# Decoder trunk on one core: every fourth weight chunk's low part comes from an accumulating GpSimd DMA

## The chip, the core and the metric

The kernel runs on one core of one Trainium2 chip. The metric is the device time of one execution in microseconds (us). The engines are TensorE (PE in the profile, its weight loads PEld), VectorE (DVE), ScalarE (ACT), GpSimd (POOL) and SyncE (SP). Each works through a queue of its own in order, and they wait for each other with semaphores. DMAs are issued from the queues of SyncE, ScalarE and GpSimd.

## What is computed

A decoder trunk of two layers over 256 tokens of width 2048, all in float32. A layer is a mixer (one input projection of 5632 columns; sliding-window attention with sinks beside a gated linear recurrence; one output projection), a SwiGLU feed forward of width 5632, and a gated per-layer embedding, with RMS norms between:

```python
for i in range(DEPTH):                     # 2
    h = rms_norm(x, pre_mix_gain[i])
    m = hybrid_mixer(h, positions, w_in[i], ..., w_out[i])
    x = x + rms_norm(m, post_mix_gain[i])
    h = rms_norm(x, pre_ffn_gain[i])
    f = (jax.nn.silu(h @ w_ffn_gate[i]) * (h @ w_ffn_up[i])) @ w_ffn_down[i]
    x = x + rms_norm(f, post_ffn_gain[i])
    gate = jax.nn.sigmoid(rms_norm(x, ple_gain[i]) @ w_ple_gate[i])
    x = x + (p[i] @ w_ple_proj[i]) * gate
```

## The kernel before

Every large product has its two operands split into a high and a low part of at most 12 significant bits each (type fp32r), and is made of three products: high by high, low by high, high by low. Lines 206, 207 and 208, in `part` inside `strip`, are these three; their accumulators are the tiles `acc`, two of them per strip, one for each token tile of 128 tokens. A strip is 512 output columns for both token tiles. It walks over its weights in chunks of two k-tiles of 512 columns (128 x 1024 elements, 512 KB), eight chunks to a strip of 2048 rows; a chunk feeds 12 matmuls. There are 840 chunks in the program.

`load_w` brings a chunk in. Its DMA on SyncE's queue (L188) writes a tile `wr`, of which there are four buffers. `split` then lets ScalarE cast it to the high part `wh` (L159), and VectorE subtract that from `wr` to give the low part `wl` (L160). Of `wh` and `wl` there are eight buffers each. So a load waits until a `wr` buffer has been read by VectorE, and a cast waits until TensorE has done with the `wh` buffer of eight chunks earlier. The inputs of the products, tiles `ck`, are made by `split_T`: TensorE transposes (L167, `ms`), ScalarE writes the high part (L175, with a gain, or L159), VectorE the low one (L176 or L160).

A scheduler that works before the launch sets the order on each engine and the buffer that each tile gets; it takes the instructions in the order of the program text, and moves one ahead when it estimates that it will be ready sooner. The text itself delays work by chunks: `later(n, fn)` writes a piece n chunks on.

Around the strips stand the pieces that take the accumulators away: rotary halves (VectorE L395, GpSimd L402), attention and recurrence, the activations of the feed forward (L697, L703), the running sum of the down projection (L721, L723), and `post_norm`, which at the end of the two output projections of a layer adds the normed result to the residual `x` (L232) and makes the next inputs. Sums of squares are ScalarE's (L155, tile `junk`), and the few steps from them to a reciprocal root are GpSimd's (L140 to L150). In the strips that follow a norm, `skew` makes the second token tile run four or five chunks behind the first.

Of the kernel before, what the change touches and what calls it, by code (L numbers as in the profile page):

```python
# [8 lines left out]
F32 = mybir.dt.float32  # L9
# [27 lines left out]
    0.0003162277571391314, 0.00023713737027719617, 0.00017782794020604342, 0.0001333521504420787,  # L37
]
PI = 3.141592653589793
BIG = (25600.0, 134.0, 1.921875, 0.005126953125, 1.6254460206255317e-05)  # 4096 * 2 pi  # L40
TWO = (6.28125, 0.0019350051879882812, 3.0199157663446385e-07)  # 2 pi
ROUND = 12582912.0  # 1.5 * 2^23


@with_exitstack
def decoder(ctx: ExitStack, tc: tile.TileContext, x, p, positions, w_in, attn_sinks,
# [19 lines left out]

    queue = []
    clock = [0]

    def later(n, fn):  # L70
        """trace fn n weight chunks from now"""
        queue.append((clock[0] + n, fn))

    running = []

    def start(gen):
        """trace gen up to its first yield, and from one yield to the next every chunk"""
        running.append(gen)
        if next(gen, True):
            running.remove(gen)  # L80
# [13 lines left out]
    def bank(shape=(P, W)):  # L94
        return pms.tile(list(shape), F32, tag="ms", name="ms")

# [1 line left out]
    xr = [[xp.tile([P, W], F32, tag=f"x{t}{s}", name=f"x{t}{s}") for s in range(4)]  # L98
          for t in range(NT)]
# [1 line left out]
    ident = cp.tile([P, P], F32, name="ident")  # L101
    make_identity(nc, ident)
    mhalf = cp.tile([P, 8], F32, name="mhalf")
    G.memset(mhalf, -0.5)

    # per-feature vectors, one feature per partition
    g0rows = cp.tile([32, P], F32, name="g0rows")
    S.dma_start(g0rows, pre_mix_gain.rearrange("l (c p) -> (l c) p", p=P))
    gT = cp.tile([P, P], F32, name="gT")
# [21 lines left out]
    def gain_cols(base, l, n):  # L131
        return gT[:, base + l * n: base + (l + 1) * n]

# [1 line left out]
    def rstd(ss, n, count=1, name="rs"):  # L135
        """(ss / n + eps) ^ -0.5, ss [P, count]"""
        v = tiny(count)
        V.tensor_scalar(v, ss, 1.0 / n, EPS, op0=ALU.mult, op1=ALU.add)
        r = sm.tile([P, count], F32, name=name)
        G.tensor_tensor(r, v, mhalf[:, 0:count], op=ALU.pow)  # L140
        return r
# [13 lines left out]
        S.activation(j[:, 0:shape[1]], src, AF.Square, accum_out=acc)  # L155

    def split(src, hi, lo):
        """src = hi + lo, each of at most 12 significant bits"""
        S.copy(hi, src)  # L159
        V.tensor_tensor(lo, src, hi.bitcast(F32), op=ALU.subtract)  # L160

    def split_T(src_blocks, gcols, hl, t, kt0=0):
        """transpose 128-wide blocks [tok, feat] and split, per-feature gain if given"""
        n = len(src_blocks)
        ps = bank((P, n, P))
        for b, blk in enumerate(src_blocks):
            T.transpose(ps[:, b], blk, ident)  # L167
        h = hl[0][:, kt0:kt0 + n, t * P:(t + 1) * P]
        lo = hl[1][:, kt0:kt0 + n, t * P:(t + 1) * P]
        if gcols is None:  # L170
            split(ps, h, lo)
            return
        for b in range(n):
            g = gcols[:, b:b + 1]
            S.activation(h[:, b], ps[:, b], AF.Copy, scale=g)  # L175
            V.scalar_tensor_tensor(lo[:, b], ps[:, b], g, h[:, b].bitcast(F32),  # L176
                                   op0=ALU.mult, op1=ALU.subtract)
# [5 lines left out]
        return [a[:, b * P:(b + 1) * P] for b in range(4)]  # L183

    def load_w(w, c, col):
        """two k-tiles of 512 columns, split"""
        raw = wpr.tile([P, 2, W], F32, tag="wr", name="wr")
        nc.sync.dma_start(raw, w[c * 2 * P:(c + 1) * 2 * P, col:col + W].rearrange(  # L188
            "(k p) n -> p k n", p=P))
        hi = wps.tile([P, 2, W], F32R, tag="wh", name="wh")  # L190
        lo = wps.tile([P, 2, W], F32R, tag="wl", name="wl")
        split(raw, hi, lo)
        return hi, lo

    def strip(lhs, w, col, done, nch=8, row0=0, skew=0, psum=None, pre=None):
        """512 output columns for both token tiles; lhs[c] = (hi, lo) of 4 k-tiles"""
        ps = psum or [pacc.tile([P, W], F32, tag="acc", name=f"acc{t}") for t in range(NT)]
        ws = {}

        def part(t, c):  # L200
            hi, lo = ws[c]
            for k in range(2):
                kt = 2 * c + k
                xh, xl = (a[:, kt % 4, t * P:(t + 1) * P] for a in lhs[kt // 4])
                first, last = kt == 0, kt == 2 * nch - 1
                T.matmul(ps[t], xh, hi[:, k], start=first, stop=False)  # L206
                T.matmul(ps[t], xl, hi[:, k], start=False, stop=False)  # L207
                T.matmul(ps[t], xh, lo[:, k], start=False, stop=last)  # L208

        for i in range(nch + skew):  # L210
            if pre:
                pre(i)
            if i < nch:
                ws[i] = load_w(w, row0 // (2 * P) + i, col)
                part(0, i)
                if i == nch - 1:
                    done(0, ps[0])
            if i >= skew:
                part(1, i - skew)
            tick()  # L220
        done(1, ps[1])
# [4 lines left out]
        return b  # L226

    def post_norm(mg, ss, t, nss, xT, gcols):
        """after the last strip of a token tile: x += mg * rstd, and the next input"""
        r = sum_rstd(ss[t], D, f"po{t}")  # L230
        for c in range(4):
            V.scalar_tensor_tensor(xr[t][c], mg[c][:, t], r[:, 0:1], xr[t][c],  # L232
                                   op0=ALU.mult, op1=ALU.add)
            next_in(t, c, xT, gcols)
        for c in range(4):
            square_sum(xr[t][c], nss[t][:, c:c + 1])
# [13 lines left out]
            return got[t]  # L250
        return get

    # ---- masks, sinks and rotary tables
    ones = cp.tile([P, P], F32, name="ones")
    m_low = cp.tile([P, P], F32, name="m_low")      # [j, i]: i >= j
    m_up = cp.tile([P, P], F32, name="m_up")        # [j, i]: i < j
    m_prev = cp.tile([P, P], F32, name="m_prev")    # [i, j]: j > i
    m_neg = cp.tile([P, P], F32, name="m_neg")      # [i, j]: j > i gives the mask value
    LEV = (1, 2, 4, 8, 16, 32, 64)  # block lengths; the last two take no mask
    m_lev = cp.tile([P, 5, 64], F32, name="m_lev")  # L260
    lb = cp.tile([P, DEPTH, 8], F32, name="lb")
    omlb = cp.tile([P, DEPTH, 8], F32, name="omlb")
# [8 lines left out]
    def constants():  # L271
# [12 lines left out]
        for li, k in enumerate(LEV[:5]):  # L284
            select(m_lev[:, li], ones[:, :64], [[-2 * k, 64 // k], [0, k]], 0, 1)
            select(m_lev[:, li], m_lev[:, li], [[2 * k, 64 // k], [0, k]], k - 1, -1)
        # lower bounds: softmax over the layers, cumulative sum minus the first
        lmax = tiny(8)
        V.tensor_copy(lmax, lbl[:, 0])
        for l in range(1, DEPTH):  # L290
# [16 lines left out]
            V.tensor_tensor(lb[:, l], lcum, lbl[:, 0], op=ALU.subtract)  # L307
            V.tensor_scalar(omlb[:, l], lb[:, l], -1.0, 1.0, op0=ALU.mult, op1=ALU.add)

        # attention sinks, on every partition  # L310
        G.dma_start(sink.rearrange("p l h -> p (l h)"),
                    attn_sinks.rearrange("l h -> (l h)").partition_broadcast(P))
        V.tensor_scalar(nsink, sink, -1.0, None, op0=ALU.mult)

        # rotary angles: token per partition
        G.dma_start(posi, positions.rearrange("o (t p) -> p (o t)", p=P))
        posf = tiny(NT)
        V.tensor_copy(posf, posi)
# [31 lines left out]
        V.tensor_scalar(ra, ra, -1.0, PI / 2, op0=ALU.mult, op1=ALU.add)  # L350
        S.activation(cos, ra, AF.Sin)

# [1 line left out]
    ss = new_ss("ssx")  # L354
    xT = [new_ck() for c in range(4)]

# [9 lines left out]
            later(4, constants)  # L366

    for l in range(DEPTH):
        # ================= mixer =======================================================
        rx = lazy_rstd(ss, "rx")  # L370
        wi = w_in[l]
        attn = [new_ck(), new_ck()]
# [15 lines left out]
            return rot[t]  # L388

        def rotate(src, tb, i, n, o1, o2):  # L390
            """src [P, n heads, 64] in PSUM; o1, o2: [P, n/4, 4, 32] views in the order (g, j)"""
            a = nat()
            b = nat()
            for d, k in ((a, i), (b, i + 1)):
                V.tensor_tensor(d[:, 0:n * 64].rearrange("p (h d) -> p h d", d=32),  # L395
                                src.rearrange("p (h d) -> p h d", d=32),
                                tb[:, k].unsqueeze(1).to_broadcast([P, 2 * n, 32]), op=ALU.mult)
            av = a[:, 0:n * 64].rearrange("p (g j two d) -> p g j two d", j=4, two=2, d=32)
            bv = b[:, 0:n * 64].rearrange("p (g j two d) -> p g j two d", j=4, two=2, d=32)
            for dst, x1, x2, op in ((o1, av[:, :, :, 0], bv[:, :, :, 1], ALU.subtract),  # L400
                                    (o2, av[:, :, :, 1], bv[:, :, :, 0], ALU.add)):
                G.tensor_tensor(dst, x1, x2, op=op)  # L402
# [51 lines left out]
                    split_T(blocks4(ao[t][:, h]), gain_cols(96, l, 8)[:, 4 * h:4 * h + 4], attn[h], t)  # L454

        def head_group(half, g, t):
            """four query heads on one key head: scores; then the exponentials' transpose; then values"""
            kv = 2 * half + g
            rows = slice(g * 64, (g + 1) * 64)
            q = qT[half]  # L460
# [49 lines left out]
            square_sum(dst, ssa[t][:, kv:kv + 1], (P, 256))  # L510

        class Rec:
            """four heads of the gated recurrence"""

            def __init__(s, grp):
                s.grp = grp
# [145 lines left out]
            strip(xT, wi, 3584 + grp * W, rec.done_i)  # L662
            strip(xT, wi, 4608 + grp * W, rec.done_g)

        # ---- output projection, post norm
        mixT = [mix[c] for c in range(4)]
        ssm = new_ss("ssm")
        ss = new_ss("ssx")
# [11 lines left out]
                    post_norm(mg, ssm, t, ss, xT, gain_cols(32, l, 16))  # L680
            strip(mixT, w_out[l], s * W, done, skew=SKEW if s == 3 else 0)

        # ================= feed forward ================================================
        rx2 = lazy_rstd(ss, "ry")
        ssf = new_ss("ssf")
        nss = new_ss("ssx")
# [44 lines left out]
            ff0 += glen  # L731
        xT, ss = nxT, nss

        # ================= gated per-layer embedding ===================================
        rp = lazy_rstd(ss, "rp")
        pT2 = sp.tile([P, 2, 2, SEQ], F32R, tag="at", name="pT2")
        pT = [pT2[:, 0], pT2[:, 1]]
# [58 lines left out]
```

## Time and profile before

| | |
|---|---|
| time, median of 3 runs | 2515.0 us (2514.89 to 2515.26) |
| span of the profiled execution | 2514.3 us, within 0.7 us of that median; the page gives no other time of this execution |
| granted TensorE clock, mean | 0.999 |
| TensorE / VectorE / ScalarE / GpSimd busy | 99% / 57% / 47% / 4% |
| weight queue of SyncE (q1) | 449.37 MB, 55.9% of the 16 DMA engines' span |

A group line of the profile has the source line, engine, operation and tiles, shapes and count; then busy time and the mean of one in ns; then the idle time of the engine ahead of it and what ended it. A line of waits has who waited for whom, the sum in us, how often, and the longest. A row of windows has its bounds, its length, busy us of each engine with counts, the granted clock, the mean share of the DMA engines and GB/s. A row of the timeline or of the chain has start and duration. The rows themselves stand in the prediction.

### The profile page before, as it was taken

What the parts mean: (1) busy time and instruction counts of PE and PEld (TensorE: products, weight loads), DVE (VectorE), ACT (ScalarE), POOL (GpSimd) and SP (SyncE); (2) the same over time, 40 slices, a digit from 0 to 9 for tenths busy, and PEclk for the clock granted to TensorE, in tenths of its full rate; (3) what the DMA queues carried; (4) which work ended last, traced back from release to release, by engine and by line L of the source; (5) the groups of instructions that cost most, each with busy time, mean ns of one, the idle gap of its engine ahead of it and who ended that gap; (6) DMA issues with size and microseconds to landing.
All of it is one profiled execution on the core that took longest, in us unless ns stands there. A gap on an engine that the chain in (4) does not pass through costs nothing.

```text
span 2514.3 us, 31017 instructions
## 1 busy us (share of the span) xinstructions
PE 2490.2 (99%) x11779; PEld 2063.0 (82%) x11779; DVE 1431.4 (57%) x1777; ACT 1179.4 (47%) x1682; POOL 95.5 (4%) x209
## 2 busy tenths in 40 slices
PE   8999999999999999999999999999999999999999
PEld 6888888888888888887888888888888888888877
DVE  6666655544455455457566766565445544554574
ACT  6554445544444434446555443464444344344463
POOL 2100001000000000001011000010000000000010
PEclk9999999999999999999999999999999999999999
DMA  7344455656556656564563454556666665566653
GB/s 253 126 135 150 152 176 167 212 190 192 191 189 190 192 192 193 185 202 167 179 202 108 151 159 143 191 163 212 189 192 192 190 189 191 193 189 193 200 177 125
DMA packets 234260, 451.43 MB, mean 180 GB/s; under 512 B 14176, under 2 KB 15104, under 8 KB 234112
## 3 DMA queue, kind: packets, MB, share of 16 engines
q1 hardware_dynamic: 233808, 449.37, 55.9%
q8 instruction: 92, 1.51, 0.2%
q14 instruction: 56, 0.46, 0.0%
q10 hardware_dynamic: 240, 0.07, 0.0%
q0 software_dynamic: 64, 0.02, 0.0%
HBM read 447.31 MB, written 2.10 MB: 179 GB/s over the span
## 4 chain that ended last, share of the span: by engine, by line
PE 93%; ACT 2%; DVE 2%; DMA 1%; POOL 1%; issue 1%; SPq 0%; DVEq 0%; ACTq 0%; POOLq 0%
PE acc L206 29%; PE acc L208 29%; PE acc L207 29%; PE ms L579 1%; PE ms L167 1%; ACT junk L155 1%; PE ms L464 1%; ACT ck L175 1%; DVE wl L160 1%; ACT wh L159 1%; DMA wr<-in_w_in_dram 1%; PE ms L505 1%; DMA wr<-in_w_ple_gate_dram 0%; PE ms L594 0%; PE ms L491 0%
## 5 line engine op out<-in xcount | busy, mean ns | idle before, releaser
L160 DVE TENSOR_TENSOR wl<-wr,wh 128x1024 fp32r<-128x1024 f32 x840 | 1029.8, 1227 | 974.8 <-ACT wh L159 954.0
L159 ACT CAST wh<-wr 128x1024 fp32r<-128x1024 f32 x840 | 884.7, 1054 | 1189.2 <-PE acc L207 1127.0
L206 PE MATMUL acc<-wh,ck 128*128 128x512 f32 x3328 | 1309.2, 394 | 5.0 <-ACT ck L175 5.0
L208 PE MATMUL acc<-wl,ck 128*128 128x512 f32 x3328 | 1301.3, 391 | 0.4 <-DVE wl L160 0.4
L207 PE MATMUL acc<-wh,ck 128*128 128x512 f32 x3328 | 1299.9, 391 | 0.0
L206 PEld LDWEIGHTS acc<-wh,ck 128*128 128x128 f32 x3328 | 626.3, 188 | 134.0 <-ACT ck L175 7.6
L208 PEld LDWEIGHTS acc<-wl,ck 128*128 128x128 f32 x3328 | 625.9, 188 | 131.6 <-DVE wl L160 1.6
L207 PEld LDWEIGHTS acc<-wh,ck 128*128 128x128 f32 x3328 | 626.3, 188 | 126.3 <-DVE ck L160 0.5
L175 ACT ACTIVATE ck<-ms,gT 128x128 fp32r<-128x128 f32 x256 | 82.6, 379 | 30.8 <-DVE ck L176 26.1
L176 DVE SCALAR_TENSOR_TENSOR ck<-ms,gT,ck 128x128 fp32r<-128x128 f32 x256 | 79.0, 345 | 17.4 <-ACT ck L175 17.0
L145 POOL TENSOR_TENSOR tiny<-ssf 128x1 f32<-128x1 f32 x4 | 2.1, 534 | 1378.2 <-ACT junk L155 1377.9
L579 PEld LDWEIGHTS ms<-q,k 128*128 128x128 f32 x320 | 38.2, 191 | 2.7 <-PE acc L208 1.7
L579 PE MATMUL ms<-q,k 128*128 128x64 f32 x320 | 38.3, 272 | 0.0
L167 PE MATMUL ms<-ident,x 128*128 128x128 f32 x192 | 31.3, 287 | 5.1 <-DVE x L232 4.1
L697 ACT ACTIVATE nat<-acc,ry 128x512 f32<-128x512 f32 x44 | 30.2, 686 | 10.7 <-PE acc L208 10.6
L155 ACT ACTIVATE junk<-x 128x512 f32<-128x512 f32 x48 | 30.5, 636 | 9.2 <-DVE x L232 3.9
L167 PEld LDWEIGHTS ms<-ident,x 128*128 128x128 f32 x192 | 23.0, 146 | 14.4 <-issue 5.4
L723 DVE TENSOR_TENSOR macc<-acc,macc 128x512 f32<-128x512 f32 x48 | 33.0, 687 | 0.7
L703 DVE SCALAR_TENSOR_TENSOR nat<-acc,ry,nat 128x512 f32<-128x512 f32 x44 | 32.4, 748 | 0.1
L160 DVE TENSOR_TENSOR ck<-ms,ck 128x512 fp32r<-128x512 f32 x44 | 30.1, 684 | 0.0
L481 ACT ACTIVATE nat<-nat,tiny 128x128 f32<-128x128 f32 x64 | 24.9, 390 | 9.0 <-DVE tiny L478 9.0
L402 POOL TENSOR_TENSOR nat<-nat 128x256 f32<-128x256 f32 (+1 forms) x24 | 23.6, 1012 | 140.5 <-PE acc L208 77.9
(184 smaller groups left out, 889.6 us busy)
## 6 DMA issues: line engine op xcount, KB each, us to landing
wr<-in_w_in_dram SPq DMA_DIRECT2D x176, 512.0 KB, 3.5
wr<-in_w_ffn_gate_dram SPq DMA_DIRECT2D x176, 512.0 KB, 3.5
wr<-in_w_ffn_up_dram SPq DMA_DIRECT2D x176, 512.0 KB, 3.5
wr<-in_w_ffn_down_dram SPq DMA_DIRECT2D x176, 512.0 KB, 3.7
wr<-in_w_out_dram SPq DMA_DIRECT2D x64, 512.0 KB, 3.7
wr<-in_w_ple_gate_dram SPq DMA_DIRECT2D x64, 512.0 KB, 4.2
wr<-in_w_ple_proj_dram SPq DMA_DIRECT2D x8, 512.0 KB, 4.6
x<-in_x_dram SPq DMA_DIRECT2D x8, 256.0 KB, 5.3
```

Source lines behind the costliest of these rows:

```text
L155: S.activation(j[:, 0:shape[1]], src, AF.Square, accum_out=acc)
L159: S.copy(hi, src)
L160: V.tensor_tensor(lo, src, hi.bitcast(F32), op=ALU.subtract)
L167: T.transpose(ps[:, b], blk, ident)
L175: S.activation(h[:, b], ps[:, b], AF.Copy, scale=g)
L176: V.scalar_tensor_tensor(lo[:, b], ps[:, b], g, h[:, b].bitcast(F32), op0=ALU.mult, op1=ALU.subtract)
L206: T.matmul(ps[t], xh, hi[:, k], start=first, stop=False)
L207: T.matmul(ps[t], xl, hi[:, k], start=False, stop=False)
L208: T.matmul(ps[t], xh, lo[:, k], start=False, stop=last)
L579: T.matmul(pl[:, t * 4 + h].rearrange("p (b k) -> p b k", k=k), s.k[:, h, t * P:(t + 1) * P], up, start=True, stop=True)
L703: V.scalar_tensor_tensor(gate[t], ps, rx2(t)[:, 0:1], gate[t], op0=ALU.mult, op1=ALU.mult)
L723: V.tensor_tensor(m, ps, m, op=ALU.add)
```

## The change

A counter `nload` numbers the chunks. For three of four nothing changes. For every fourth one (indices 3, 7, 11 and so on) ScalarE makes the high part as before, then ScalarE also writes its negative into `lo`, and a DMA on GpSimd's queue adds the whole `raw` chunk onto it. VectorE has no part in these 210 chunks. Beside that the changed file has its comments removed; line numbers after the counter are one higher, and in `load_w` and after it up to seven higher.

```diff
+    nload = [0]
 ...
         hi = wps.tile([P, 2, W], F32R, tag="wh", name="wh")
         lo = wps.tile([P, 2, W], F32R, tag="wl", name="wl")
-        split(raw, hi, lo)
+        nload[0] += 1
+        if nload[0] % 4:
+            split(raw, hi, lo)
+        else:
+            S.copy(hi, raw)
+            S.mul(lo, hi.bitcast(F32), -1.0)
+            G.dma_start(lo, raw, accum_op=ALU.add)
         return hi, lo
```

Two places of the order, both in the feed forward of the first layer. Numbers at names tell buffers apart, and a bracket has the semaphores that a row waits for: DMAHW of SyncE's and ScalarE's DMAs, DMASW of GpSimd's, the others of engines.

ScalarE, before:

```order
L159 CAST wh_7248<-wr_7246 128x1024 [waits DMAHW7_49,DVE_49,PE_49]
L159 CAST wh_7270<-wr_7268 128x1024 [waits DMAHW0_49,DVE_49,PE_49]
L159 CAST wh_7288<-wr_7286 128x1024 [waits DMAHW1_49,DVE_49,PE_49]
L159 CAST wh_7306<-wr_7304 128x1024 [waits DMAHW2_49,DVE_49,PE_49]
L159 CAST wh_7324<-wr_7322 128x1024 [waits DMAHW3_49,DVE_49,PE_49]
```

ScalarE, after; the chunks of `wr_6854` and `wr_6927` are fourth ones:

```order
L197 CAST wh_6856<-wr_6854 128x1024 [waits DMAHW7_49,PE_49]
L198 ACTIVATE wl_6857<-wh_6856 128x1024 [waits DMASW4_49,PE_49,Activation_49]
L160 CAST wh_6875<-wr_6873 128x1024 [waits DMAHW0_49,DVE_49,PE_49]
L160 CAST wh_6893<-wr_6891 128x1024 [waits DMAHW1_49,DVE_49,PE_49]
L160 CAST wh_6911<-wr_6909 128x1024 [waits DMAHW2_49,DVE_49,PE_49]
L197 CAST wh_6929<-wr_6927 128x1024 [waits DMAHW3_49,PE_49]
```

The multiplication stands right behind its cast and ahead of the next chunk's cast.

SyncE's loads, before:

```order
L188 DMA wr_6804<-in_w_ffn_gate_dram 128x2x512 [waits DMAHW4_49,DVE_49]
L188 DMA wr_6822<-in_w_ffn_gate_dram 128x2x512 [waits DMAHW5_49,DVE_49]
L188 DMA wr_6840<-in_w_ffn_gate_dram 128x2x512 [waits DMAHW6_49,DVE_49]
L188 DMA wr_6858<-in_w_ffn_gate_dram 128x2x512 [waits DMAHW7_49,DVE_49]
L188 DMA wr_6882<-in_w_ffn_up_dram 128x2x512 [waits DMAHW0_49,DVE_49]
```

After, from one fourth chunk to the load that takes its buffer:

```order
L189 DMA wr_6854<-in_w_ffn_gate_dram 128x2x512 [waits DMAHW4_49,DVE_49]
L189 DMA wr_6873<-in_w_ffn_gate_dram 128x2x512 [waits DMAHW3_49,DMASW5_49]
L189 DMA wr_6891<-in_w_ffn_gate_dram 128x2x512 [waits DMAHW5_49,DVE_49]
L189 DMA wr_6909<-in_w_ffn_gate_dram 128x2x512 [waits DMAHW6_49,DVE_49]
L189 DMA wr_6927<-in_w_ffn_gate_dram 128x2x512 [waits DMAHW0_49,DVE_49]
L189 DMA wr_6952<-in_w_ffn_up_dram 128x2x512 [waits DMAHW7_49,DMASW6_49]
```

Before, each load waits for VectorE's reading of the chunk four loads earlier. After, one in four waits for a GpSimd DMA: `wr_6952`, the fifth load behind `wr_6854`, has that chunk's address, while the fourth, `wr_6927`, has the address of `wr_6873`.

On GpSimd 210 rows of `L199 DMA wl<-wr` are new, spread among the sums of the norms and the rotary halves. On TensorE the matmuls at the starts and around the norms stand in a slightly other order; in the strips of the feed forward they stand as before.

## The prediction

> **What bounds the kernel now.** I read the page's head first, for who is busy.
>
> ```profile
> span 2514.3 us, 31017 instructions
> PE 2490.2 (99%) x11779; PEld 2063.0 (82%) x11779; DVE 1431.4 (57%) x1777; ACT 1179.4 (47%) x1682; POOL 95.5 (4%) x209
> q1 hardware_dynamic: 233808, 449.37, 55.9%
> ```
>
> TensorE is busy 99% of the span; VectorE, ScalarE and the weight queue (q1) are at about half. The span is 0.7 us under the median of the three runs (2515.0), so a sum made against the span is read against the median as it stands. Next the costliest groups, and then the waits of every engine, for whether any of this half load ends late.
>
> ```profile
> L160 DVE TENSOR_TENSOR wl<-wr,wh 128x1024 fp32r<-128x1024 f32 x840 | 1029.8, 1227 | 974.8 <-ACT wh L159 954.0
> L159 ACT CAST wh<-wr 128x1024 fp32r<-128x1024 f32 x840 | 884.7, 1054 | 1189.2 <-PE acc L207 1127.0
> ```
>
> ```profile
> ACT wh L159 <- PE acc L207: 1127.0, 705, 7.2
> DVE wl L160 <- ACT wh L159: 954.0, 698, 8.3
> ```
>
> ```profile
> PE acc L206 <- ACT ck L175: 5.0, 3, 4.6
> PE ms L167 <- DVE x L232: 4.1, 6, 1.1
> PE ms L111 <- DMA g0rows<-in_pre_mix_gain_dram: 3.7, 1, 3.7
> PE ms L414 <- POOL nat L402: 2.9, 1, 2.9
> PE ms L531 <- DVE ck L176: 1.7, 2, 0.9
> PE ms L167 <- DVE x L756: 0.8, 2, 0.5
> PE acc L208 <- DVE wl L160: 0.4, 2, 0.2
> ```
>
> ScalarE's cast waits for TensorE to give back a wh buffer, in 705 of 840 chunks: the eight wh/wl pairs are full, and the split runs a whole ring ahead. VectorE only follows ScalarE. TensorE has waited 0.4 us in all for a low part. The timeline of the feed forward shows the beat.
>
> ```profile
> 703.69 1.05 ACT L159 CAST wh<-wr 128x1024 fp32r<-128x1024 f32 x1 [1.65 <-PE acc L207]
> 706.41 1.05 ACT L159 CAST wh<-wr 128x1024 fp32r<-128x1024 f32 x1 [1.67 <-PE acc L207]
> ```
>
> ```profile
> 704.78 1.22 DVE L160 TENSOR_TENSOR wl<-wr,wh 128x1024 fp32r<-128x1024 f32 x1 [1.37 <-ACT wh L159]
> ```
>
> ```profile
> L188 SPq DMA_DIRECT2D wr<-in_w_ffn_down_dram x8: 367/368/368, 702.8 to 722.3; - x8
> DMA to landing us min/median/max: 3.6/3.7/3.8
> ```
>
> One chunk takes 2.72 us, four take 10.88. VectorE starts 1.09 us after its cast and ends 2.31 us after it; then the wr buffer is free, and the next load lands 3.7 us after its issue. When a cast starts, seven chunks lie ahead of it on TensorE: 7 x 2.72 = 19.0 us, and its first low product is two matmuls further on (two times 2.72/12, so 0.45). So a low part is done 19.5 - 2.3 = 17.2 us before its use.
>
> **The change part by part.** VectorE loses 210 of its 840 subtractions: 210 x 1.227 = 257.7 us, which takes it from 57% to 47%. This is off the path (17.2 us of lead, 0.4 us of waits), so it is worth 0 in steady state.
>
> ScalarE gains 210 multiplications of 128x1024. No row has that form; the same shape is the cast at 1.054, and the dearest reading is two halves of the scaled activation:
>
> ```profile
> L697 ACT ACTIVATE nat<-acc,ry 128x512 f32<-128x512 f32 x44 | 30.2, 686 | 10.7 <-PE acc L208 10.6
> ```
>
> Two of those are 1.37. I take 1.1, nearer to the cast, which also reads and writes SBUF: 231 us, so 47% becomes 56%. It stands in the 1.67 us that ScalarE idles ahead of each cast. If that cover goes (start and norms, below), each costs up to 1.1.
>
> The GpSimd queue gains 210 issues, and the transfers share the 16 engines with the loads. The only rows on that queue, beside small loads of ScalarE's queue in the same first microseconds, are these:
>
> ```profile
> grows<-in_ple_gain_dram ACTq DMA_DIRECT2D x1, 16.0 KB, 4.1
> sink<-in_attn_sinks_dram POOLq DMA_DIRECT2D x1, 16.0 KB, 6.0
> posi<-in_positions_dram POOLq DMA_DIRECT2D x1, 1.0 KB, 5.8
> ```
>
> ```profile
> 6.24 0.78 POOL L311 DMA_DIRECT2D sink<-in_attn_sinks_dram  x1
> ```
>
> An issue of 0.78 makes 164 us, 4% becomes 10%. Let X be the time from issue to landing of an accumulating DMA of 512 KB, which the trace doesn't show. Lower end: 3.7, a load of that size. Upper end: 6.0 (the sink's, same queue and 128 partitions) and two passes of the bytes, since source and destination are both read: q1 moved 449.37 MB in 55.9% of 2514.3 us, 320 GB/s, so 0.524 MB take 1.64 us, and X is 6.0 + 3.3 = 9.3. I take 6.0 + 1.6 = 7.6: the sink's row is the nearest, being on the same queue.
>
> The Trainium skill ("DMA: Bandwidth & Descriptors", Anatomy of one DMA) fits such a transfer as 2.0 us plus its bytes at 436 GB/s, and gives some 1 us more to the first byte: by that X would be an estimated 4.2, the sum below would stay, and the rival of the slot ring would have no chance. The 5.8 us of a 1 KB load here speaks against it, so that rival keeps its chance.
>
> Three things must hold for X to be hidden.
>
> First, lead: cast 1.09, multiplication 1.1, hand-over 0.06, so the DMA starts 2.25 us after the cast, and TensorE wants the result at 19.5. That holds up to X = 17.2.
>
> Second, wr comes back later, at 2.25 + X. The order of SyncE shows the load that then waits: it is the fifth after it and not the fourth, since the built program gives the slot of the chunk behind it (freed by VectorE) to the fourth. Of 208 such reuses 183 are at distance five, 19 at four, 6 at six or seven. The ring is then: DMA (X), load (3.7), cast and subtraction (2.31), the load three chunks on into that slot (3.7), cast and multiplication (2.25), and again a DMA, eight chunks later. 12.0 + X must fit in 8 x 2.72 = 21.8 us: it holds up to X = 9.8, and with 7.6 there are 2.2 us over. A distance of four (2.25 + X + 3.7 within 10.88, so X up to 4.9) makes one cast 2.7 us late, which the lead covers.
>
> Third, engines: the loads use
>
> ```profile
> 500.00:700.00 200.00, 200.00 (x897) 165.38 (x896) 98.55 (x88) 87.30 (x93) 0.00 (x0) 1.00 0.60 191
> ```
>
> 60% of the 16 engines (last but one column), 6.5 of 10.88 us. The transfer adds 1.6 to 3.3, so 75% to 90%.
>
> On GpSimd the sums for the norms (L145 to L150) and the rotary halves (L402) now stand behind DMAs that wait for ScalarE's multiplication. In the order a DMA ahead of them belongs to a chunk that is split when TensorE frees its buffer, about when they become ready themselves; so each is held for the 0.78 us of an issue at most, while TensorE works on the other token tile: 0. If that cover is gone, it is 0.78 at each norm, within the losses of the next paragraph.
>
> What is left is the start and the norms, where the lead is used up. The chain of waits in the first embedding stage:
>
> ```profile
> 1172.32 3.60 DMA wr<-in_w_ple_proj_dram
> 1177.56 1.23 DVE wl L160
> 1178.84 5.38 DMA wr<-in_w_ple_gate_dram
> ```
>
> A subtraction of VectorE, late behind its norm work, holds the next load. That chunk is a fourth one (index 391), so its low part now leaves VectorE's queue. Of the waits of TensorE above, those on VectorE and on the rotary halves are 4.1 + 2.9 + 1.7 + 0.8 + 0.4 = 9.9 us; that is the most that a lighter VectorE can give. Against it ScalarE's 1.1 us stands about eleven times in such places (three at the start, two at each of four norms), 12 us at most, since ScalarE is busy there too:
>
> ```profile
> 1156.00:1196.00 40.00, 38.30 (x183) 29.73 (x182) 35.38 (x66) 32.13 (x75) 6.41 (x14) 1.00 0.50 173
> ```
>
> VectorE 35.4 and ScalarE 32.1 of 40 us: VectorE is the fuller, so I take 4 us of gain and 2 of loss.
>
> Sum: 2515.0 + 0 (VectorE) + 0 (ScalarE) + 0 (GpSimd) + 0 (X hidden) - 4 + 2 = 2513.
>
> **The rivals.** About 0.2% (5 us) is what a measurement of this kernel can tell from no change.
>
> *Hidden, no change*, as above: 2510 to 2520.
>
> *The lighter VectorE counts* at the start and norms: up to 9.9 us, 2505 to 2510. For it: VectorE holds the chain there. Against it: of TensorE's waits only 0.4 us are on a low part, and ScalarE takes up most of the work.
>
> *ScalarE is late at the start and norms*: up to 12 us, 2520 to 2540 with some lateness of the first DMAs. For it: the longest wait of TensorE after the first load, 4.6, is on ScalarE (first of the rows of PE above). Against it: VectorE is the fuller there.
>
> *The slot ring binds*, the one on the other side: from X = 9.8 in unbroken strips. In two long stretches
>
> ```profile
> 310.00:1263.00 953.00, 409.91 (x335) 353.78 (x336) 1.00 0.59 187
> 1574.00:2490.00 916.00, 401.46 (x328) 345.95 (x328) 1.00 0.60 190
> ```
>
> (windows of the tile wr: VectorE, then ScalarE) stand 664 casts, 166 fours in 1869 us, 11.26 us each. A ring of 12.0 + X is for eight chunks; beyond X = 10.5 each us adds 0.5 x 166 = 83 us. X = 13 gives 2720. For it: the sink's 6.0 for 16 KB, and loads that come more slowly beside the transfers (each us on the 3.7 counts twice in the ring). Against it: 2.2 us of room.
>
> *The DMA engines bind*: the accumulation needs over 10.88 - 6.5 = 4.4 us of all 16 engines. At 6 us, four chunks take 12.5, and (12.5 - 11.26) x 166 = 206 us come on top: 2720. For it: no row shows what adding in flight costs. Against it: two passes are 3.3. The Trainium skill ("DMA: Bandwidth & Descriptors", Issuing engines are not separate DMA queues) says that transfers of all issuers run interleaved on the same 16 engines, the rule behind this rival; no run here shows it yet.
>
> **How the numbers follow.** No change 0.36, lighter VectorE 0.26, late ScalarE 0.14, slot ring 0.14, engines 0.10. Faster is 0.26, same 0.36, slower 0.38. The likeliest gives 2513, its own range is 2508 to 2520. The range for 8 in 10 starts at 2505 (9.9 us of gain) and goes to 2690, just under the two binding rivals' 2720 at the values taken, with half their chance inside.
>
> **What would show it.** Right: VectorE near 1174 us, ScalarE near 1410, casts still waiting for TensorE, GpSimd's DMA landing in 6 to 9.3 us, engine share under 0.9 in the feed forward, four chunks in 10.88 us. Wrong: loads of SyncE that wait for that DMA for long, TensorE waiting at its third product (the low part's) in the feed forward, casts that wait for wr instead of TensorE, a landing over 10 us, or an engine share at 1.

## The result and the profile after

The changed kernel takes 2537.3 us (median of 4 runs, 2535.8 to 2541.6) against 2515.1 us for the kernel before, run beside it: ratio 1.0084, 95% interval 1.0072 to 1.0096. It is slower by 0.84%, some 22 us, where the prediction said 2513.

First the head of the page after, the busy times and the two large DMA queues (q1 the weight loads, q0 the GpSimd DMAs).

```profile
span 2533.4 us, 31466 instructions
PE 2496.0 (99%) x11779; PEld 2064.7 (81%) x11779; DVE 1178.4 (47%) x1567; ACT 1385.9 (55%) x1892; POOL 259.6 (10%) x419
q1 hardware_dynamic: 233808, 449.37, 53.7%
q0 software_dynamic: 30304, 110.13, 24.6%
```

The work moved as announced: VectorE fell by 253 us, ScalarE rose by 207, GpSimd by 164. The span is 19.1 us longer. TensorE's idle time (span less busy) went from 24.1 to 37.4 us, which is 13.3 of the 19.1; the other 5.8 stand as longer busy time of the same 11779 matmuls. (The medians are 22 us apart, 3 more than the two profiled executions; those 3 are not pursued.)

What the new instructions cost, from the groups (busy, mean ns, then idle before and its releaser) and from the list of DMA issues (KB, median us to landing):

```profile
L199 POOL DMA_DIRECT2D wl<-wr x210 | 179.5, 855 | 1968.0 <-ACT wl L198 1551.3
L198 ACT ACTIVATE wl<-wh 128x1024 fp32r<-128x1024 f32 x210 | 222.3, 1058 | 4.3
wl<-wr POOLq DMA_DIRECT2D x210, 512.0 KB, 4.8
wr<-in_w_ffn_gate_dram SPq DMA_DIRECT2D x176, 512.0 KB, 4.3
```

The accumulating DMA lands 4.8 us after its issue, with 3.7 as the lower bound and 7.6 as the value taken. It costs 24.6% of 2533.4 us over 210 transfers, 2.97 us of all 16 engines each.

Now the waits of TensorE, the list that showed 0.4 us for low parts before:

```profile
PE acc L215 <- DMA wl<-wr: 8.7, 5, 2.9
PE acc L213 <- ACT ck L176: 7.6, 2, 4.6
...
PE ms L168 <- DVE x L763: 3.0, 1, 3.0
```

The first row is new: the low-part product (L215) waits for the GpSimd DMA, but only for 5 of the 210 chunks. These are 127 and 547 (in the first feed forward strip of either layer; 2.7 and 2.9 us) and 391, 395 and 811 (in the embedding stages; 1.2, 1.1 and 0.7). The long stretch of the feed forward is as forecast. Its window (busy of PE, PEld, VectorE, ScalarE, GpSimd, then clock, engine share, GB/s) shows TensorE busy throughout, the 16 engines at 0.85 and a full clock:

```profile
500.00:700.00 200.00, 200.00 (x895) 165.46 (x894) 73.93 (x66) 107.15 (x113) 15.29 (x18) 1.00 0.85 238
```

So the time must be lost at a few places. To find them I compared, for each weight chunk, the start of its first low-part product in the two traces. For chunk 144 (counted from 0), in the timelines of before and then of after:

```profile
496.22 0.39 PE L208 MATMUL acc<-wl,ck 128*128 128x512 f32 x1
```

```profile
503.52 0.39 PE L215 MATMUL acc<-wl,ck 128*128 128x512 f32 x1
```

After is 7.3 us late there. The same difference at nine chunks, in us, for this kernel and for those below (each one profiled execution; negative is ahead of before):

| kernel | 32 | 112 | 144 | 376 | 416 | 512 | 576 | 784 | 832 |
|---|---|---|---|---|---|---|---|---|---|
| after | 2.4 | 2.3 | 7.3 | 7.3 | 14.3 | 13.9 | 17.5 | 17.5 | 19.0 |
| e1_steady | -0.7 | -0.8 | -0.8 | -0.8 | -0.5 | -0.9 | -0.9 | -0.9 | -0.9 |
| e2_edges | 3.9 | 3.9 | 7.2 | 7.2 | 12.6 | 12.7 | 17.7 | 17.7 | 18.9 |
| e3_dveadd | -4.5 | -4.3 | -4.6 | -4.6 | -4.8 | -3.4 | -3.8 | -3.8 | -3.0 |
| e4_plain | -0.6 | -0.6 | 0.8 | 0.8 | 1.7 | 2.9 | 5.1 | 5.1 | 5.5 |
| e5_room4 | 6.8 | 6.8 | 10.2 | 10.3 | 17.7 | 17.3 | 22.4 | 22.5 | 24.5 |
| e6_room5 | 1.9 | 1.9 | 5.5 | 5.6 | 7.9 | 7.6 | 12.3 | 12.4 | 14.3 |
| e7_scratch | 5.1 | 4.9 | 4.6 | 4.7 | 10.1 | 9.5 | 9.9 | 10.0 | 9.7 |
| e9_start | -5.2 | -5.2 | -5.2 | -5.2 | -5.0 | -4.9 | -5.0 | -5.0 | -4.9 |
| e10_mix | -4.2 | -4.2 | -4.6 | -4.6 | -4.7 | -3.5 | -3.9 | -3.9 | -3.1 |

In the first row the long stretches (32 to 112, 144 to 376, 576 to 784) lose nothing. The loss comes in steps: 2.4 us at the start, 5.0 at the feed forward's start in layer 0 (112 to 144), 7.0 in layer 0's embedding stage (376 to 416), 3.6 at layer 1's feed forward start, 1.5 in its embedding stage.

The step at chunk 127, the fourth chunk at the first feed forward's start, can be followed row by row. Before (ScalarE's cast, VectorE's subtraction, TensorE's use):

```profile
430.89 1.14 ACT L159 CAST wh<-wr 128x1024 fp32r<-128x1024 f32 x1
439.27 1.22 DVE L160 TENSOR_TENSOR wl<-wr,wh 128x1024 fp32r<-128x1024 f32 x1
442.22 0.39 PE L208 MATMUL acc<-wl,ck 128*128 128x512 f32 x1
```

After (cast, negative, DMA issue, use; in brackets the idle time before a row and what ended it):

```profile
439.96 1.10 ACT L197 CAST wh<-wr 128x1024 fp32r<-128x1024 f32 x1
441.67 1.12 ACT L198 ACTIVATE wl<-wh 128x1024 fp32r<-128x1024 f32 x1
443.09 0.89 POOL L199 DMA_DIRECT2D wl<-wr  x1 [2.23 <-ACT wl L198]
449.17 0.79 PE L215 MATMUL acc<-wl,ck 128*128 128x512 f32 x1 [2.72 <-DMA wl<-wr]
```

Before, the low part was done at 440.49 and used at 442.22: a lead of 1.7 us here, not the 17.2 us of the steady beat. The norm work on ScalarE and VectorE has used the lead up. After, cast and negative stand among the same norm work (the cast now 9.1 us later than before, behind most of it in ScalarE's order), and from the start of the negative to the use lie 7.5 us (1.42 to the issue, 6.08 from there to the use). TensorE stood ready at 446.45.

In layer 0's embedding stage the way is a longer one. The chain of waits of after, in order of time (start, us, what):

```profile
1214.44 1.07 ACT wl L198
...
1215.80 6.01 DMA wl<-wr
...
1221.83 3.96 DMA wr<-in_w_ple_gate_dram
...
1225.87 1.05 ACT wh L160
...
1226.95 1.23 DVE wl L161
1228.17 0.61 DVE nat L762
...
1228.80 0.70 DVE x L763
```

Chunk 403's accumulating DMA holds its load buffer until 1221.81. Only then is the load of chunk 408 issued, five chunks on; its cast and VectorE's subtraction follow, and the stage's residual (L762, L763) stands behind that subtraction in VectorE's queue. TensorE needs the residual for its transposes, and TensorE's row shows what it waited:

```profile
1229.55 0.66 PE L168 MATMUL ms<-ident,x 128*128 128x128 f32 x4 [2.96 <-DVE x L763]
```

The DMA's own low part was in time here; it is the buffer that came back too late. So there are two suspects: the low part that is late itself (chunk 127), and the load buffer that is held longer (chunk 403).

Chunk 391, which the prediction counted as a gain because its subtraction would leave VectorE's busy queue, shows both. Its rows in after:

```profile
1168.03 0.37 SPq L189 DMA_DIRECT2D wr<-in_w_ple_gate_dram  x1
1173.48 1.11 ACT L197 CAST wh<-wr 128x1024 fp32r<-128x1024 f32 x1
1181.50 1.12 ACT L198 ACTIVATE wl<-wh 128x1024 fp32r<-128x1024 f32 x1
1188.86 0.50 PE L215 MATMUL acc<-wl,ck 128*128 128x512 f32 x1 [1.23 <-DMA wl<-wr]
```

and its load before:

```profile
1155.15 0.37 SPq L188 DMA_DIRECT2D wr<-in_w_ple_gate_dram  x1
```

The load is issued 12.9 us later at a place that was 7.3 us late so far; the negative comes 8.0 us after its cast, behind norm work on ScalarE; and the use follows 7.4 us after the negative's start. Before, VectorE had this low part at 1178.8 (the chain shown with the prediction).

Last, the clock. After the two waits of some 3 us shown above (2.72 and 2.96), the first two windows here (clock in the last column but two) give TensorE half its clock. The third window lies behind the wait of 2.92 us at chunk 547 and has the full clock:

```profile
449.00:452.00 3.00, 2.83 (x7) 2.25 (x8) 0.00 (x0) 0.68 (x1) 0.00 (x0) 0.53 0.78 244
1231.00:1234.00 3.00, 3.00 (x8) 2.20 (x7) 1.40 (x4) 1.39 (x3) 0.00 (x0) 0.50 0.73 234
1707.00:1710.00 3.00, 3.00 (x13) 2.48 (x14) 0.00 (x0) 1.77 (x2) 0.00 (x0) 1.00 0.77 225
```

Seven or eight matmuls in 3 us instead of 13: the first two waits cost another 1.5 to 1.7 us each behind themselves, the third costs nothing more. So a wait of this length may be followed by half clock and need not be; what decides it is open. Adding (1 - clock) over windows of 2 us from 8 us to TensorE's last matmul gives 6.8 us lost in after and 3.4 in before, so 3.4 of the 5.8 us of longer busy time are the clock. The wait of 1.23 us at chunk 391 has no such stretch behind it. The Trainium skill ("TensorE: Matmul & The Clock Gate", What's actually happening) halves the clock after about 3.4 us of idling and gives it back after as long a busy stretch. The trace agrees on the second: the windows 449.2 to 452.5 and 1230.9 to 1234.2 are at 0.50 throughout, and the full clock follows. On the first it differs: here waits of 2.72 and 2.96 us were enough.

### The profile page after: what moved, and what is told of

Read it like the earlier page. It is cut to its first block, busy times and chain, and to the rows that moved or that the text cites. A ratio compares the mean times of both kernels' runs of the same rounds, so it can differ in the third digit from the quotient of the medians.

```text
span 2533.4 us, 31466 instructions
## 1 busy us (share of the span) xinstructions
PE 2496.0 (99%) x11779; PEld 2064.7 (81%) x11779; DVE 1178.4 (47%) x1567; ACT 1385.9 (55%) x1892; POOL 259.6 (10%) x419
## 3 DMA queue, kind: packets, MB, share of 16 engines
q1 hardware_dynamic: 233808, 449.37, 53.7%
q0 software_dynamic: 30304, 110.13, 24.6%
## 4 chain that ended last, share of the span: by engine, by line
PE 92%; DMA 3%; ACT 2%; issue 1%; DVE 1%; POOL 1%; SPq 0%; POOLq 0%; DVEq 0%; ACTq 0%
PE acc L213 28%; PE acc L215 28%; PE acc L214 28%; DMA wl<-wr 2%; PE ms L586 1%; PE ms L168 1%; ACT ck L176 1%; PE ms L471 1%; ACT junk L156 1%; DMA wr<-in_w_in_dram 1%; PE ms L512 1%; DVE x L239 1%; PE ms L601 0%; ACT wh L160 0%; PE ms L498 0%
## 5 line engine op out<-in xcount | busy, mean ns | idle before, releaser
L161 DVE TENSOR_TENSOR wl<-wr,wh 128x1024 fp32r<-128x1024 f32 x630 | 772.7, 1228 | 1184.0 <-ACT wh L160 1164.0
L215 PE MATMUL acc<-wl,ck 128*128 128x512 f32 x3328 | 1303.0, 392 | 9.2 <-DMA wl<-wr 8.7
L215 PEld LDWEIGHTS acc<-wl,ck 128*128 128x128 f32 x3328 | 626.6, 188 | 143.1 <-DMA wl<-wr 11.1
L199 POOL DMA_DIRECT2D wl<-wr x210 | 179.5, 855 | 1968.0 <-ACT wl L198 1551.3
L198 ACT ACTIVATE wl<-wh 128x1024 fp32r<-128x1024 f32 x210 | 222.3, 1058 | 4.3
L168 PEld LDWEIGHTS ms<-ident,x 128*128 128x128 f32 x192 | 22.5, 147 | 18.8 <-issue 6.5
```

The source lines that it names most:

```text
L198: S.mul(lo, hi.bitcast(F32), -1.0)
L199: G.dma_start(lo, raw, accum_op=ALU.add)
```

## The experiments

The theory: the loss arises only where TensorE's lead over the split is drained (the start, the feed forward starts, the embedding stages), through the DMA's landing there. The rivals: the transfers cost a little everywhere through shared engines; or ScalarE's extra work is what hurts; and, within the theory, low part late against buffer held.

**e1_steady: the DMA in the long stretches only.** The 34 fourth chunks near the start and the norms are split by VectorE, 176 keep the new path.

```diff
-        if nload[0] % 4:
+        near = any(a <= nload[0] - 1 < b for a, b in
+                   ((0, 24), (112, 136), (376, 412), (536, 560), (796, 824)))
+        if nload[0] % 4 or near:
```

> The GpSimd path is left out for the 34 fourth chunks at the start and around the four norms (chunk indices 0 to 23, 112 to 135, 376 to 411, 536 to 559, 796 to 823); the other 176 keep it. Theory A (the low part comes too late only where the lead of eight buffers is used up): the loss of 22 us goes, 2513 to 2518, and TensorE's waits for the low part by DMA are about 0. Theory B (a cost that every such chunk pays: ScalarE's work, transfers beside loads): 176/210 of 22 us stay, about 2533.

2515.8 us, ratio 0.9999 [0.9990, 1.0007]. Its DMA rows:

```profile
q0 software_dynamic: 25408, 92.30, 20.8%
wl<-wr POOLq DMA_DIRECT2D x176, 512.0 KB, 4.8
```

176 transfers with the same landing, a fifth of the engines' time, and no time lost: steady sharing costs nothing. Nothing is won either, though VectorE is lighter by 214 us.

**e2_edges: the complement.** Only those 34 chunks take the new path.

```diff
-        if nload[0] % 4:
+        if nload[0] % 4 or not near:
```

> The complement: only the 34 fourth chunks at the start and the four norms take the GpSimd path. Theory A: the loss stays nearly whole, 2530 to 2537, with TensorE's waits for the low part by DMA of some 8 us as in the changed kernel. Theory B: 34/210 of 22 us, about 2519.

2536.2 us, ratio 1.0084 [1.0071, 1.0098]: 34 of 210 chunks carry the whole loss, and its steps in the table come at the same places as in after, with 17.7 against 17.5 us at chunk 576 (single steps differ by up to 1.7 us, one stretch of half clock, which e2's trace has at the third step and not at the first two). From its waits and its DMA issues:

```profile
PE acc L216 <- DMA wl<-wr: 7.8, 5, 2.7
wl<-wr POOLq DMA_DIRECT2D x34, 512.0 KB, 5.9
```

At these places the DMA also takes longer, 5.9 us.

**e3_dveadd: ScalarE's new work without the DMA.** ScalarE casts and negates as in the changed kernel, VectorE adds.

```diff
-            G.dma_start(lo, raw, accum_op=ALU.add)
+            V.tensor_tensor(lo, raw, lo.bitcast(F32), op=ALU.add)
```

> Every fourth chunk keeps ScalarE's cast and negative, but VectorE adds the chunk onto it; no DMA. It leaves ScalarE's added work and its place in the queue, and takes away the DMA's time and traffic. Theory A1 (the DMA's 4.8 us and its hold on the load buffer make the low part late): 2515 to 2520. Theory A2 (the added ScalarE work at the norms, where it holds up the next inputs and the cast behind it, makes it late): 2530 or more.

2512.2 us, ratio 0.9986 [0.9977, 0.9995]. With all of the new ScalarE work the kernel is not slower but a little faster than before, and 3 us under the range of theory A1, the nearer one: ScalarE's 210 negatives by themselves are no cause. Chunk 127 shows what is. Its negative and VectorE's addition:

```profile
433.77 1.12 ACT L198 ACTIVATE wl<-wh 128x1024 fp32r<-128x1024 f32 x1
434.93 1.23 DVE L199 TENSOR_TENSOR wl<-wr,wl 128x1024 fp32r<-128x1024 f32 x1
```

The negative stands behind norm work here, too, but 2.4 us after its start the low part is done, where the DMA's way took 7.5, and TensorE does not wait. The cause is the DMA in the chain.

**e4_plain: the DMA without adding.** The transfer copies the chunk into the low part's buffer and adds nothing, so the low part is the whole chunk; the number of transfers, their bytes and the waits stay.

```diff
-            G.dma_start(lo, raw, accum_op=ALU.add)
+            G.dma_start(lo, raw)
```

> The GpSimd DMA copies the chunk onto the low part without adding (the low part is then the whole chunk, so the products are others); all else as in the changed kernel. If the adding itself is dear, it lands well under 4.8 us, its queue's share falls from 24.6% to about 13%, and the time falls to 2525 or less. If it is the path of cast, negative and a GpSimd DMA as such: 2532 to 2537 with a landing over 4 us.

2522.9 us, ratio 1.0033 [1.0020, 1.0045].

```profile
q0 software_dynamic: 30304, 110.13, 12.0%
wl<-wr POOLq DMA_DIRECT2D x210, 512.0 KB, 2.9
```

The same bytes take half the engine time (12.0% of 2519.8 us over 210, 1.44 us each, against 2.97) and land in 2.9 us; an issue holds GpSimd 0.54 us instead of 0.86. With 1.9 us less of landing the steps shrink to 1.4 and 2.2 at the feed forward starts (5.0 and 3.6 in after) and 0.9 in layer 0's embedding stage (7.0); 13.6 of the 19.1 us of span are gone, 3 of them at the start, which also moves by itself (see e9).

**e5_room4 and e6_room5: a fifth load buffer.** Room for it is made by placing start constants and rotary scratch in shared buffers and by 12 instead of 16 small ones. e5 has this with four load buffers, as the control for e6 and e7; e6 has five.

```diff
-    wpr = ctx.enter_context(tc.tile_pool(name="wpr", bufs=4))
+    wpr = ctx.enter_context(tc.tile_pool(name="wpr", bufs=5))
```

> Control for the next two: the changed kernel with room made in SBUF (start-up constants share buffers that are used later, 12 small tiles and not 16); still four load buffers. As the changed kernel, 2530 to 2542, but for the start, whose order can move by some us.

> The same with five load buffers, so that the load behind a fourth chunk's DMA waits for a buffer one chunk less. Theory H (the loss comes by the load buffer, which the DMA holds longer, so that later loads and casts start late): the loss falls by half or more against the control, to 2525 or less. Theory L (the low part itself is late, by the 4.8 us of the DMA behind cast and negative): at most 3 us less than the control.

e5: 2540.7 us, 1.0100 [1.0085, 1.0116]. e6: 2532.0 us, 1.0068 [1.0051, 1.0085]: 8.7 us less than the control, more than theory L allows and less than theory H asks. The fifth buffer takes 7.4 us in layer 0's embedding stage down to 2.3 and the start from 6.8 to 1.9, but nothing at the feed forward starts (3.4 and 3.7; 5.1 and 4.7). TensorE's wait for the DMA stays (9.0 us in the control):

```profile
PE acc L216 <- DMA wl<-wr: 8.9, 5, 2.9
```

So the held buffer costs in the embedding stage and perhaps at the start, and the late low part costs at the feed forward starts. (The kernel before was not run with five load buffers, so what a fifth one gives without the change is not known; e7 tests the same question in another way.)

**e7_scratch: hold the buffer, keep the low part on VectorE.** VectorE makes every low part; ScalarE's negative goes to a scratch tile and the DMA adds the chunk there, so the chunk's load buffer is held as in the changed kernel, but TensorE doesn't need the transfer. The control is e5.

```diff
-            S.copy(hi, raw)
-            S.mul(lo, hi.bitcast(F32), -1.0)
-            G.dma_start(lo, raw, accum_op=ALU.add)
+            split(raw, hi, lo)
+            S.mul(scr, hi.bitcast(F32), -1.0)
+            G.dma_start(scr, raw, accum_op=ALU.add)
```

> All that the change adds, but without use: VectorE makes every low part as before; for every fourth chunk ScalarE also writes the negative into a scratch tile, and the GpSimd DMA adds the chunk onto that, with the same hold of the load buffer and the same traffic. Theory L: 2513 to 2520, and no wait of TensorE for a DMA. Theory H, or the traffic: 2530 or more.

2524.0 us, ratio 1.0035 [1.0022, 1.0048], again between the two theories. It is the mirror of e6: nothing lost at the feed forward starts (-0.3 and 0.4, against 3.4 and 5.1 in the control), 5.4 us still lost in the embedding stage (7.4 in the control). There the chain of waits is that of after with the scratch tile in it, although nobody needs the scratch:

```profile
1210.77 5.69 DMA scr<-wr
...
1216.47 4.71 DMA wr<-in_w_ple_gate_dram
...
1222.34 1.23 DVE wl L162
1223.57 0.61 DVE nat L765
...
1224.20 0.70 DVE x L766
```

and TensorE's wait for that residual is 4.8 us:

```profile
PE ms L169 <- DVE x L766: 4.8, 1, 4.8
```

Both suspects have a part, each at its own place. In e7, too, GpSimd's sums for the norms stand among the new issues, and the feed forward starts lose nothing, so GpSimd's queue is no cause there.

**e8_half: every second chunk**, 420 transfers, to find out how far the engines are from their limit.

```diff
-        if nload[0] % 4:
+        if nload[0] % 2:
```

> Every second chunk takes the GpSimd path. By the trace of the changed kernel one such DMA takes 24.6% of 2533 us over 210, or 2.97 us of all 16 engines; 420 of them and the loads (53.7%) are 2607 us of engine time. If the engines then bind: 2620 to 2800 with an engine share of 0.95 or more in the feed forward, and four chunks no longer in 10.88 us. If only the lead at the norms counts: 2540 to 2570 with four chunks still in 10.88 us.

2737.2 us (2 runs), ratio 1.0883 [1.0848, 1.0918]. The window of the feed forward and the DMA issue:

```profile
700.00:900.00 200.00, 190.82 (x838) 157.04 (x837) 54.30 (x54) 111.77 (x114) 29.20 (x34) 0.97 0.99 266
wl<-wr POOLq DMA_DIRECT2D x420, 512.0 KB, 6.6
```

The share (last but one) is 0.99, the landing grows to 6.6 and TensorE is no longer full. Here the 16 engines bind. By the rows of after this was to be expected: 53.7% of 2533.4 us over 857 units of 512 KB (449.37 MB) is 1.59 us for a load, so four chunks need 4 x 1.59 + 2.97 = 9.3 us of 10.88 with one such transfer, and 12.3 with two; in this window they take 11.8. The Trainium skill ("DMA: Bandwidth & Descriptors", Issuing engines are not separate DMA queues) says that all issuers share these engines; the 0.99 agrees.

**e9_start and e10_mix: where e3's gain is, and the best of both.** e9 does e3's edit for the six fourth chunks of the first 24 alone; all others are split as before. e10 has the accumulating DMA in the 176 chunks of e1 and e3's addition in the other 34.

```diff
-        if nload[0] % 4:
+        if nload[0] % 4 or nload[0] > 24:
...
-            G.dma_start(lo, raw, accum_op=ALU.add)
+            V.tensor_tensor(lo, raw, lo.bitcast(F32), op=ALU.add)
```

```diff
+            if near:
+                V.tensor_tensor(lo, raw, lo.bitcast(F32), op=ALU.add)
+            else:
+                G.dma_start(lo, raw, accum_op=ALU.add)
```

> Only the six fourth chunks among the first 24 are changed, and without a DMA: ScalarE casts and negates, VectorE adds; all other chunks are split as in the kernel before. Open is where the earlier run with this form in all 210 chunks got its gain of about 3 us. If at the start alone, where another order of the first instructions spares 4 to 5 us: 2509 to 2513. If the moved work matters at the later norms too, or the gain was that of one lucky order: 2514 to 2517, no change.

> The 176 fourth chunks of the long stretches keep cast, negative and accumulating DMA of the changed kernel; the 34 at the start, the feed forward starts and the embedding stages take cast and negative on ScalarE and the addition on VectorE. If the DMA costs only where the lead is drained, this is at 2511 to 2516, at or below the kernel before; if the negative's place in ScalarE's queue is what hurts at those 34 chunks, 2520 to 2530. If it gives 2512 like the form without any DMA, the 176 DMAs are free and win nothing.

e9: 2513.4 us, ratio 0.9992 [0.9983, 1.0001]; the interval touches 1, so whether it is faster isn't shown, and 2513.4 lies between the two forecasts. Its profiled execution is 5 us ahead of before from chunk 32 on and stays there; that execution (span 2509.4) was the shortest of 11 runs from 2511.2 to 2517.2, so part of the 5 us may be chance. e10: 2512.5 us, 0.9987 [0.9979, 0.9996], the same as e3's 0.9986. In the traces of e3 and e10, too, the gain is there by chunk 32. All three lack the 2.9 us wait for the rotary halves that TensorE has before (quoted with the prediction), and none has a stretch of half clock in the first 100 us, of which before has two, some 3.4 us lost. The second of them, with no wait of TensorE from 60 us on ahead of it, reads

```profile
84.00:87.00 3.00, 3.00 (x8) 2.35 (x8) 0.73 (x1) 0.21 (x1) 0.00 (x0) 0.50 0.55 178
```

What e10 adds is that 176 accumulating DMAs on top of e3's form neither cost nor win: e3, without any, is as fast. The best versions seen, e3 and e10, are 0.14% faster than the kernel before. Their gain comes from the start and not from a lighter VectorE in the long stretches; how much of it is the changed order of the first instructions and how much the clock of a single execution is not shown.

## Why the prediction failed

**The step that failed** is the last term, "start and the norms", taken as a gain of 4 and a loss of 2 us. It was a loss of 19 us of span. The prediction used the right fact, that the lead is used up there, and priced VectorE's relief (up to 9.9 us) against 1.1 us of ScalarE's time in eleven places. It left out that the moved low part keeps its whole new chain at those places: ScalarE's queue for the negative, GpSimd's issue, and X. "X hidden" rested on 17.2 us of lead, read in the feed forward; at chunk 127 the lead was 1.7 us, and it stood in the trace of before; the new way from the negative to the low part took 7.5 us there. Chunk 391 was read as proof that VectorE was the late one; by the new way its load and its low part came later still.

The second thing left out there is the buffer. The prediction worked out that it comes back later by 2.25 + X and tested that against the ring of the long stretches, where there is room; in the embedding stage, where the chain from buffer to residual has none, e6 and e7 show it as some 5 us. The third is the half clock behind two of the waits, 3.4 us in all, which the prediction did not count though before has such stretches, too.

The time of 2537 us does lie inside the range that the prediction gave, 2505 to 2690, but by luck: the upper part of that range stood there for the slot ring and the DMA engines as limits, and in after neither limits (share 0.85, casts that wait for TensorE).

**The rival "ScalarE is late at the start and norms"** gave 2520 to 2540, and 2537 lies in that. It had the right places and size, and by its words "some lateness of the first DMAs" a part of the cause, but the wrong engine: e3 keeps all of ScalarE's added work and loses nothing. The main loss is the DMA's time behind that work.

**X** was taken as 7.6 and measured 4.8, and 5.9 for the 34 chunks of e2. The sink's 6.0 for 16 KB was a poor neighbour. The page cited with it ("DMA: Bandwidth & Descriptors" of the Trainium skill) gave an estimated 4.2, nearer to the 4.8 than my value; its fit alone (2.0 us plus the bytes at 436 GB/s), without the 1 us that was added to it, is an estimated 3.2, and e4's transfer without adding landed in 2.9. Over-estimating X didn't help the sum, since X was set to nothing by the cover.

**Engine load, the ring and the beat** held. VectorE was forecast at 1174 and is at 1178; ScalarE at 1410 and is at 1386; the negative at 1.1 and took 1.058; the issue at 0.78 and took 0.855; the engine share at 0.75 to 0.90 and was 0.85. ScalarE's casts still wait for TensorE: this is the row that "the ring has room" predicted.

```profile
ACT wh L160 <- PE acc L214: 676.2, 473, 6.4
```

Of the signs given for a wrong forecast two appeared. TensorE waited at its third product in the feed forward (chunks 127 and 547), and this was a true sign. The other appeared without meaning a loss: SyncE's loads wait long for the DMA.

```profile
SPq L189 <- DMA wl<-wr: 571.2, 206, 13.5
```

571 us of waiting in 206 loads; e1 still has 440 us of it in 172 loads and loses nothing. A queue's long wait tells of loss only where the engine behind it has no lead. The loads themselves slowed from 3.5 us to 4.3 (medians of the rows of `w_ffn_gate`) beside the transfers, for which the ring has room since X is 4.8.

**VectorE's 257.7 us at no worth** was right: e1 takes 214 us off VectorE and runs at 0.9999.

**What stays open.** The start moved by -5 to +7 us among these kernels; order and room change there together, and why a given order is better is not settled. The split of layer 0's embedding step in after between buffer and late low part is not exact (without the late low part e7 keeps 5.4 of its control's 7.4 us; with the fifth buffer e6 loses 5.1 of them). Of the longer busy time of TensorE, 2.4 us are not explained by the clock. Why one wait of some 3 us is followed by half clock and another is not stays open, too.

## What to carry to other kernels

A latency is hidden by the lead at the place where it is paid, not by the lead of the steady beat: before giving work a longer chain, read the lead at each stage change, from the end of the producer's row to the consumer's row. Relieving VectorE, which was not the bound, won nothing here (e1, e10), so this offload could only lose; one that has another use should leave out the pieces at the edges. When a total is off by a little, comparing the same instruction's time in both traces, piece by piece, shows at once whether it is lost in steps or at a slope.

## What was not expected of the hardware

Adding during the transfer doubles its engine time: 2.97 us of all 16 engines for 512 KB within SBUF against 1.44 us for the plain copy, and 4.8 against 2.9 us to landing (e4). At 420 such transfers the engines are full (share 0.99) and the kernel is 8.8% slower. And a wait of TensorE of some 3 us can cost more than its own length: half clock for 3 us and more, 1.5 to 1.7 us lost. It need not: in after the waits of 2.72 and 2.96 us were followed by half clock and the one of 2.92 was not, nor was one of 3.21 us in e2. The kernel before has such a stretch from 84 to 87 us, with no wait of TensorE from 60 us on.
